# A two-layer decoder trunk: tokens 128 to 255 of layer 0 stored in reverse order

## Chip, cores and metric

The kernel runs on one core of a Trainium2 chip, in one launch. The metric is the device time of that launch in microseconds (us). All inputs and outputs are float32 in the chip's main memory.

## The reference

256 tokens of width 2048 pass through two layers and a last norm. Layer 0 mixes tokens by two recurrences side by side, layer 1 by attention; each layer ends with a squared-ReLU MLP. The change touches layer 0 alone:

```python
proj = rms_norm(x) @ w_in                       # 2048 -> 6144
x_lru, y_lru, q_h, f_h, v_h, g_h = jnp.split(proj, ...)
lru = rg_lru(causal_depthwise_conv(x_lru, ...)) * gelu(y_lru)     # 1024 wide
hg = hgrn2(q_h, f_h, v_h, g_h)                                    # 8 heads of 128
h = x + concatenate([lru, hg]) @ w_out
...
# hgrn2, per head, with q = silu(q_h), f = lb + (1 - lb) sigmoid(f_h), k = (1 - lb) sigmoid(-f_h):
decay = jnp.exp(b[:, :, :, None, :] - b[:, :, None, :, :])        # b: running sum of log f
scores = jnp.einsum('bhtk,bhsk,bhtsk->bhts', qc, kc, decay)       # causal: s <= t
o = jnp.einsum('bhts,bhsv->bhtv', scores, vc)
```

The score of query token t and key token s is a sum over 128 features, each with a decay of its own, the product of f over the tokens between them.

## The kernel before

**The stream of weights.** Nearly all the work is matrix products with streamed weights. A weight tile of 128x2048 (a unit) is loaded by SyncE (`raw`), rounded by ScalarE (ACT) into `hi`, and the rest `lo = raw - hi` is made by VectorE (DVE). TensorE (PE) multiplies three times: rounded activations by `hi` and by `lo`, the activations' rest by `hi`. `hi` and `lo` have three buffers each, so the rounding of a unit waits until PE has finished the unit three before it. In layer 0's input projection a unit is 24 matmuls of 512 columns; a group is four units and 512 output columns, in two PSUM tiles `p`, which ACT copies out to `tk`. The groups come in the order `v0 x0 x1 q0 G0 f0 q1 f1 G1 v1 g0 y0 g1 y1`, where G0 and G1 are the gates of the RG-LRU.

**The ticks.** The token mixing of layer 0 is cut into generator steps that are put between these matmuls. The table `TICKS` says, for every half unit, which lanes take a step: a and b are two pairs of HGRN2 heads each (`hgrn`), c the RG-LRU's inputs and outputs, e its scan (`lru_scan`), d the HGRN2's norm and output gate (`finish`). All of PE's matmuls are chained in the order in which the program writes them, and through layer 0's mixing so are DVE's and ACT's instructions (`InOrder`). What an engine does therefore stands in a fixed queue, and an instruction that waits holds up all behind it.

**The scores by levels.** `hgrn(c2)` handles two heads at once. Features lie on the partitions, 256 tokens along the row. Level c (1, 2, 4 to 128) joins pairs of neighbouring blocks of c tokens: keys of the first block meet queries of the second. Before level c each key has been multiplied by f of all tokens after it in its block and each query by f of all up to itself, so that one matmul gives the scores. Levels up to 16 run one matmul per head and half of the tokens (128 keys against the 64 queries in second blocks), so four per pair of heads; DVE puts the wanted blocks into the 128x128 score tiles `st` under a mask (`copy_predicated`). Levels 32 and 64 first gather the keys of first blocks of both halves into one contiguous tile `kc` (ACT), and run one matmul of 128 keys by 128 queries per head; ACT copies the blocks out to `st`. After each level DVE multiplies keys and queries by block products (`both_`) and forms the products of the next level (`nt`, in `xall`). Keys, queries and products lie in slots of the tile `xall`, so the profile calls all of these xall.

A step of lanes a and b stands every second tick, 24 matmuls apart: the transposed queries, the transposed forget gates (`f`), the diagonal (`pd`), and then the levels. Lanes a and b go through it twice: the first round is heads 0 to 3 (levels 1 to 32 at 140 to 177 us of the span), the second heads 4 to 7 (229 to 266 us). A step for both lanes together is called a block below. After level 128, the last step multiplies `st` by the values (`pd<-tk,st`).

Of the kernel before, what the change touches and what calls it, by code (L numbers as in the profile page):

```python
# [10 lines left out]
F32 = mybir.dt.float32  # L11
# [5 lines left out]
OP = mybir.AluOpType  # L17
# [3 lines left out]
P = 128  # L21
# [17 lines left out]


@with_exitstack
def trunk_kernel(ctx, tc, head, x, xtok, cols, tab, masks, pos, fin, w_in, w_gate, w_out, w_qkv, w_o, w1, w2, out):
# [361 lines left out]

    halfs.append(square(0))
    vfirst = tokens_group("v0", by_k=True, behind=halfs[1:])
    load = after(nc.sync.dma_start(xres[:, 1], xtok[:, 1]), loads)
    for d, f in ((tab_, tab), (msk, masks)):
        load = after(nc.sync.dma_start(d, f), [load])
    square(1)  # L410
# [80 lines left out]
    done = {"v0": vfirst}  # L491
    outs, roots, rooms = {}, {}, {}

    def turned(name, tiles, at):
        p = psc.tile([P, 2, S], F32, name=name, bufs=2 if name == "pl" else 1)
        for i, (z, m) in enumerate(zip(tiles, at)):
            for j in range(2):
                turn(p[:, i, j * P:j * P + P], z[:, j, m * P:m * P + P])
        return p

    def halves(t, c, second):
        return t.rearrange("p (n two c) -> p n two c", two=2, c=c)[:, :, int(second), :]

    def hgrn(c2):
        g, at = c2 // 2, 2 * (c2 % 2)
        bank = "pt" if at else "pd"
        heads = (2 * c2, 2 * c2 + 1)
        slot = 2048 * (c2 % 2)
        qk = xall[:, slot:slot + 1024].rearrange("p (t h s) -> p t h s", h=2, t=2)
        qp, kq = qk[:, 0], qk[:, 1]  # L510
        f = xall[:, slot + 1024:slot + 1536].rearrange("p (h s) -> p h s", h=2)
        rest = [slot + 1536]
        p = turned(bank, [done[f"q{g}"]] * 2, (at, at + 1))
        lut(qp, p, AF.Sigmoid)
        for h, hd in enumerate(heads):
            V.scalar_tensor_tensor(qp[:, h], p[:, h], omlb[:, hd:hd + 1], qp[:, h], op0=OP.mult, op1=OP.mult)
        yield
        p = turned("pl", [done[f"f{g}"]] * 2, (at, at + 1))
        lut(f, p, AF.Sigmoid)
        lut(kq, p, AF.Sigmoid, scale=-1.0)  # L520
        for h, hd in enumerate(heads):
            A.activation(f[:, h], f[:, h], AF.Identity, scale=omlb[:, hd:hd + 1], bias=lb[:, hd:hd + 1])
        yield
        pd = psc.tile([P, 2, 2, P], F32, name=bank, bufs=1)
        for h in range(2):
            for j in range(2):
                js = slice(j * P, j * P + P)
                mm(pd[:, h, j], kq[:, h, js], qp[:, h, js], start=True, stop=True)
        st = wk.tile([P, 2, 3, P], F32, name="st", bufs=2)
        V.tensor_tensor(st[:, :, :2], pd, ident[:, None, None, :].to_broadcast([P, 2, 2, P]), OP.mult)  # L530
        stf = st[:, :, :2].rearrange("p h a b -> p h (a b)")
        V.tensor_tensor(qp, qp, f, OP.mult)
        c = 1
        tot = f
        while c <= 128:
            yield
            pl = psc.tile([P, 2, 2, 64], F32, name="pl", bufs=2)
            plf = pl.rearrange("p h j c -> p h (j c)")
            if c == 128:
                for h in range(2):  # L540
                    mm(plf[:, h], kq[:, h, :P], qp[:, h, P:], start=True, stop=True)
                A.copy(st[:, :, 2], plf)
                break
            if c >= 32:
                for h in range(2):
                    mm(plf[:, h], kc[:, h], halves(qp[:, h], c, True), start=True, stop=True)
            else:
                for h in range(2):
                    for j in range(2):
                        js = slice(j * P, j * P + P)  # L550
                        mm(pl[:, h, j], kq[:, h, js], halves(qp[:, h, js], c, True), start=True, stop=True)
            if c <= 16:
                lv = LEVELS.index(c)
                V.copy_predicated(stf.rearrange("p h (n two c) -> p h n two c", two=2, c=c)[:, :, :, 1],
                                  msk[:, lv].rearrange("p (n c) -> p n c", c=c)[:, None].to_broadcast([P, 2, P // c, c]),
                                  pl.rearrange("p h j (n c) -> p h (j n) c", c=c))
            else:
                for n in range(P // c):
                    j, at_ = divmod(2 * n * c, P)
                    ns = slice(n * c, n * c + c)  # L560
                    A.copy(st[at_:at_ + c, :, j, at_ + c:at_ + 2 * c], plf[ns, :, ns])
            n = S // (2 * c)
            tt = tot.rearrange("p h (n two) -> p h n two", two=2)
            both_ = bass.AP(tensor=qk.tensor, offset=qk.offset + c,
                            ap=[list(qk.ap[0]), [2 * S - c, 2], [2 * c, 2 * n], [1, c]])
            fac = bass.AP(tensor=tot.tensor, offset=tot.offset,
                          ap=[list(tot.ap[0]), [1, 2], [2, 2 * n], [0, c]])
            V.tensor_tensor(both_, both_, fac, OP.mult)
            nt = xall[:, rest[0]:rest[0] + 2 * n].rearrange("p (h n) -> p h n", h=2)
            rest[0] += 2 * n  # L570
            V.tensor_tensor(nt, tt[:, :, :, 0], tt[:, :, :, 1], OP.mult)
            tot = nt
            c *= 2
            if c in (32, 64):
                at_ = slot + 1024 + 256 * (c == 64)
                kc = xall[:, at_:at_ + 256].rearrange("p (h s) -> p h s", h=2)
                A.copy(kc.rearrange("p h (n c) -> p h n c", c=c),
                       kq.rearrange("p h (n two c) -> p h n two c", two=2, c=c)[:, :, :, 0])
        yield
        vg = done[f"v{g}"]  # L580
        po = psc.tile([P, 2, 2, P], F32, name=bank, bufs=1)
        for h in range(2):
            vs = slice((at + h) * P, (at + h) * P + P)
            mm(po[:, h, 0], st[:, h, 0], vg[:, 0, vs], start=True, stop=True)
            mm(po[:, h, 1], st[:, h, 2], vg[:, 0, vs], start=True, stop=False)
            mm(po[:, h, 1], st[:, h, 1], vg[:, 1, vs], start=False, stop=True)
        if not at:
            roots[g] = wk.tile([P, 8], F32, name="hs", bufs=2)
        o = wk.tile([P, 2, 2, P], F32, name="ho", bufs=4)
        for h in range(2):  # L590
            for j in range(2):
                n = 2 * (at + h) + j
                A.activation(o[:, h, j], po[:, h, j], AF.Square, accum_out=roots[g][:, n:n + 1])
            outs[heads[h]] = o[:, h]
        A.copy(o, po)
        yield

    def finish(g, half):
# [6 lines left out]
        pair_ = [2 * half, 2 * half + 1]  # L605
        for at in pair_:
            o, z = outs[4 * g + at], done[f"g{g}"][:, :, at * P:at * P + P]
            s = wk.tile([P, 2, P], F32, name="g", bufs=2)
            lut(s, z, AF.Sigmoid)
            V.tensor_tensor(s, s, z, OP.mult)  # L610
            for j in range(2):
                V.scalar_tensor_tensor(o[:, j], o[:, j], roots[g][:, 2 * at + j:2 * at + j + 1], s[:, j],
                                       op0=OP.mult, op1=OP.mult)
        yield
        p = turned("po", [outs[4 * g + at] for at in pair_], (0, 0))
        if g and not half:
            bufb.tiles[3] = act.tile([P, 4, 2 * S], F32R, name="bufb3")
        for i, at in enumerate(pair_):
# [4 lines left out]

    def lru_in(n, half):
        b0 = 4 * n + 2 * half
        p = turned("po", [done[f"x{n}"]] * 2, (2 * half, 2 * half + 1))
# [51 lines left out]

    def lru_out(n, half):
        b0 = 4 * n + 2 * half  # L680
        p = turned("pt" if half else "pd", [done[f"y{n}"]] * 2, (2 * half, 2 * half + 1))
# [524 lines left out]
def _tables():  # L1206
# [27 lines left out]
def _layout(a):  # L1234
# [21 lines left out]
    for g in range(0, 16, 4):  # L1256
# [9 lines left out]
    return {  # L1266
        "head": c(head), "x": c(xf[:, 8:]),
        "xtok": c(n(a["x"]).reshape(2, P, D).transpose(1, 0, 2)),
        "cols": c(np.concatenate(cols, axis=1)),
        "tab": tab, "masks": masks,  # L1270
        "pos": c(n(a["positions"]).reshape(2, P).T),
# [23 lines left out]
```

## Time and profile before

| | |
|---|---|
| median of 3 runs | 2126.55 us (2126.04 to 2126.66) |
| the profiled execution | 2126.42 us |
| its span in the profile | 2124.6 us |
| PE, matmuls busy | 2115.1 us (100%) |
| DVE busy | 1780.3 us (84%) |
| ACT busy | 1310.4 us (62%) |
| granted TensorE clock | 0.999 of full speed |

The span is the time from the first to the last instruction that the profile shows; the execution's own time is 1.8 us longer. PE is TensorE's matmuls, PEld its weight loads, which overlap them. An arrow `p<-hi,bufa` means that tile p is written from hi and bufa. Line L241 is the helper `mm`, L244 the helper `turn` (a transpose on PE), and L68 the helper through which all DVE and ACT instructions go. A float32 matmul shows as two rows, since PE makes two passes of it. In a timeline a row has its start, its length and what it does; a number in brackets is the idle time of that engine before it and what ended it.

### The profile page before, as it was taken

Reading aid. Unit: us, or ns where it says so; the run is one execution under the profiler, and the core shown is the slowest. Engines: PE = TensorE matmul, PEld = TensorE weight load, DVE = VectorE, ACT = ScalarE, POOL = GpSimd, SP = SyncE. Lnnn points to the kernel's source line nnn. Section 1 sums busy time; section 2 is a strip of 40 time slices with the busy share of each in tenths; the row PEclk is TensorE's granted clock in tenths of the full one; section 3 lists DMA queues with packets and bytes.
Section 4 is the critical chain, followed back from the end, with each engine's and each line's share of the span. In section 5 each row is a group of like instructions: output and inputs, shape, how many; then the busy total and the mean of one; then the engine's idle time right before and its main releaser. Section 6 shows DMA issues by size and latency. Waiting matters only on the chain.

```text
span 2124.6 us, 24870 instructions
## 1 busy us (share of the span) xinstructions
PE 2115.1 (100%) x9828; PEld 1762.8 (83%) x9828; DVE 1780.3 (84%) x1687; ACT 1310.4 (62%) x1325; POOL 72.3 (3%) x89
## 2 busy tenths in 40 slices
PE   9999999999999999999999999999999999999998
PEld 8888888888888888888888888888888888888887
DVE  7676768988888888888998888798988987988897
ACT  7556466666566466566665666566755655755664
POOL 0000000000000000000000000000000000000000
PEclk9999999999999999999999999999999999999999
DMA  8544446887888878787788667567788778787885
GB/s 344 179 165 152 159 180 216 240 271 242 246 249 261 250 243 258 257 255 231 249 262 249 218 208 231 196 220 242 235 252 279 234 244 271 242 256 239 271 263 158
DMA packets 70164, 500.12 MB, mean 235 GB/s; under 512 B 7840, under 2 KB 8096, under 8 KB 10272
## 3 DMA queue, kind: packets, MB, share of 16 engines
q1 hardware_dynamic: 57888, 412.99, 51.1%
q0 software_dynamic: 11872, 84.94, 21.7%
q8 instruction: 77, 1.26, 0.2%
q10 hardware_dynamic: 288, 0.61, 0.1%
q14 instruction: 39, 0.32, 0.0%
HBM read 496.41 MB, written 2.10 MB: 235 GB/s over the span
## 4 chain that ended last, share of the span: by engine, by line
PE 98%; DVE 1%; ACT 1%; DMA 0%; issue 0%
PE p L241 61%; PE pd L241 15%; PE po L241 14%; PE pt L241 3%; PE pl L244 2%; PE pl L241 2%; ACT hi L68 0%; DVE lo L68 0%; DMA both_in<-in_head 0%; ACT tk L68 0%; DVE tk L68 0%; PE po L244 0%; DVE ho L68 0%; PE pd L244 0%; DVE g L68 0%
## 5 line engine op out<-in xcount | busy, mean ns | idle before, releaser
L68 DVE TENSOR_TENSOR lo<-raw,hi 128x2048 fp32r<-128x2048 f32 (+1 forms) x364 | 789.3, 2172 | 233.5 <-ACT hi L68 232.3
L68 ACT CAST hi<-raw 128x2048 fp32r<-128x2048 f32 (+1 forms) x364 | 659.3, 1817 | 500.6 <-PE p L241 309.5
L241 PE MATMUL p<-hi,bufa 128*128 128x512 f32 x2000 | 643.5, 393 | 0.2 <-ACT bufa L68 0.2
L241 PEld LDWEIGHTS p<-hi,bufa 128*128 128x128 f32 x2000 | 375.5, 188 | 77.6 <-ACT bufa L68 0.4
L241 PE MATMUL p<-hi,bufb 128*128 128x512 f32 x1264 | 405.0, 391 | 0.0
L241 PE MATMUL p<-lo,bufa 128*128 128x512 f32 x1000 | 389.4, 389 | 0.0
L68 DVE TENSOR_TENSOR lo<-s,hi 128x2048 fp32r<-128x2048 f32 x120 | 274.3, 2286 | 11.4 <-ACT hi L68 8.8
L241 PEld LDWEIGHTS p<-hi,bufb 128*128 128x128 f32 x1264 | 237.3, 188 | 48.8
L68 ACT CAST hi<-s 128x2048 fp32r<-128x2048 f32 x120 | 229.6, 1913 | 51.6 <-PE po L241 22.5
L241 PE MATMUL p<-lo,bufb 128*128 128x512 f32 x632 | 246.0, 389 | 0.0
L241 PEld LDWEIGHTS p<-lo,bufa 128*128 128x128 f32 x1000 | 187.9, 188 | 38.0 <-DVE lo L68 0.3
L241 PEld LDWEIGHTS p<-lo,bufb 128*128 128x128 f32 x632 | 118.7, 188 | 24.3
L241 PE MATMUL pd<-hi,bufa 128*128 128x512 f32 x352 | 116.8, 393 | 0.0
L241 PE MATMUL p<-hi,formx 128*128 128x512 f32 x352 | 116.3, 391 | 0.0
L68 DVE TENSOR_TENSOR lo<-t,hi 128x2048 fp32r<-128x2048 f32 x40 | 91.5, 2288 | 15.8 <-ACT hi L68 15.8
L241 PE MATMUL po<-hi,bufb 128*128 128x512 f32 (+1 forms) x320 | 102.4, 386 | 0.0
L241 PE MATMUL p<-hi,formh 128*128 128x512 f32 x288 | 94.5, 389 | 0.0
L68 DVE TENSOR_TENSOR s<-s,raw 128x2048 f32<-128x2048 f32 x40 | 91.3, 2284 | 0.5 <-DMA raw<-in_w_qkv 0.5
L68 DVE TENSOR_TENSOR s<-raw,t 128x2048 f32<-128x2048 f32 x40 | 91.5, 2286 | 0.2 <-DMA raw<-in_w_o 0.2
L68 ACT ACTIVATE y<-y 128x512 f32<-128x512 f32 x112 | 68.8, 629 | 28.0 <-DVE y L68 27.2
L241 PE MATMUL po<-hi,bufa 128*128 128x512 f32 x256 | 84.9, 393 | 0.0
L68 ACT CAST hi<-t 128x2048 fp32r<-128x2048 f32 x40 | 76.5, 1914 | 11.7 <-PE pd L241 6.0
(296 smaller groups left out, 2789.1 us busy)
## 6 DMA issues: line engine op xcount, KB each, us to landing
raw<-in_w SPq DMA_DIRECT2D x224, 1024.0 KB, 6.6
raw<-in_w_in SPq DMA_DIRECT2D x45, 1024.0 KB, 4.8
raw<-in_w_qkv SPq DMA_DIRECT2D x42, 1024.0 KB, 6.7
t<-in_w SPq DMA_DIRECT2D x32, 1024.0 KB, 6.8
t<-in_w POOLq DMA_DIRECT2D x32, 1024.0 KB, 8.9
s<-in_w POOLq DMA_DIRECT2D x32, 1024.0 KB, 9.2
raw<-in_w_out SPq DMA_DIRECT2D x15, 1024.0 KB, 4.9
raw<-in_w_o SPq DMA_DIRECT2D x15, 1024.0 KB, 4.8
```

What stands on the lines that cost most here:

```text
L68: i = call(*args, **kw)
L241: chain[:] = [after(T.matmul(*args, **kw), chain)]
L244: chain[:] = [after(T.transpose(out_, in_, ident), chain)]
```

## The change

Tokens 128 to 255 are stored backwards through layer 0's mixing: the host reverses them in the features' copy of x and in `xback` (1 MB, loaded in the place of the second half of `xtok`). In the reversed half the later block of a pair comes first. The layout of keys and queries is set so that at each level the wanted keys of both halves can be gathered into one tile `kc` of 128 columns, and the 64 queries of each half are read by one access pattern: levels 1 to 16 now run as 32 and 64 did, one matmul per head with 128 keys by 128 queries. For this ACT gathers `kc` at every level (two copies of 128 elements per lane, the function `gather`), and the sigmoid of the keys is written in two halves. The masked copies of levels 1 to 16 become two of half the size, one for each half of the tokens. `both_` now stands ahead of the masked copies. The transposes of `turned(..., back=True)` (in `lru_in`, `lru_out` and `finish`) write the second half in reverse, so that the RG-LRU and the output projection see the tokens in order. `finish` takes its scratch tile from pool tmp (`z`) and no longer from wk (`g`). The order of PE's matmuls for the weights and the ticks are unchanged.

```diff
-    load = after(nc.sync.dma_start(xres[:, 1], xtok[:, 1]), loads)
+    load = after(nc.sync.dma_start(xres[:, 1], xback), loads)
...
     done = {"v0": vfirst}
     outs, roots, rooms = {}, {}, {}
 
-    def turned(name, tiles, at):
+    def turned(name, tiles, at, back=False):
         p = psc.tile([P, 2, S], F32, name=name, bufs=2 if name == "pl" else 1)
         for i, (z, m) in enumerate(zip(tiles, at)):
             for j in range(2):
-                turn(p[:, i, j * P:j * P + P], z[:, j, m * P:m * P + P])
+                to = p[:, i, j * P:j * P + P]
+                turn(to[:, ::-1] if back and j else to, z[:, j, m * P:m * P + P])
         return p
-
-    def halves(t, c, second):
-        return t.rearrange("p (n two c) -> p n two c", two=2, c=c)[:, :, int(second), :]
 
     def hgrn(c2):
         g, at = c2 // 2, 2 * (c2 % 2)
...
         heads = (2 * c2, 2 * c2 + 1)
         slot = 2048 * (c2 % 2)
         qk = xall[:, slot:slot + 1024].rearrange("p (t h s) -> p t h s", h=2, t=2)
-        qp, kq = qk[:, 0], qk[:, 1]
+        view = lambda t, at_, *dims: bass.AP(tensor=t.tensor, offset=t.offset + at_, ap=[list(t.ap[0])] + [list(d) for d in dims])
+        queries = view(qk, 0, (S, 2), (2 * S + P, 2), (1, P))
+        keys = (qk[:, 1, :, :P], qk[:, 0, :, P:])
         f = xall[:, slot + 1024:slot + 1536].rearrange("p (h s) -> p h s", h=2)
+        by_half = lambda t: t.rearrange("p h (j s) -> p h j s", j=2)
         rest = [slot + 1536]
         p = turned(bank, [done[f"q{g}"]] * 2, (at, at + 1))
-        lut(qp, p, AF.Sigmoid)
+        lut(queries, by_half(p), AF.Sigmoid)
         for h, hd in enumerate(heads):
-            V.scalar_tensor_tensor(qp[:, h], p[:, h], omlb[:, hd:hd + 1], qp[:, h], op0=OP.mult, op1=OP.mult)
+            V.scalar_tensor_tensor(queries[:, h], by_half(p)[:, h], omlb[:, hd:hd + 1], queries[:, h], op0=OP.mult, op1=OP.mult)
         yield
         p = turned("pl", [done[f"f{g}"]] * 2, (at, at + 1))
         lut(f, p, AF.Sigmoid)
-        lut(kq, p, AF.Sigmoid, scale=-1.0)
+        for j in range(2):
+            lut(keys[j], by_half(p)[:, :, j], AF.Sigmoid, scale=-1.0)
         for h, hd in enumerate(heads):
             A.activation(f[:, h], f[:, h], AF.Identity, scale=omlb[:, hd:hd + 1], bias=lb[:, hd:hd + 1])
+        kc = wk.tile([P, 2, P], F32, name="kc", bufs=2)
+
+        def gather(c):
+            pairs_ = lambda t: t.rearrange("p h (n two c) -> p h n two c", two=2, c=c)
+            for j in range(2):
+                A.copy(pairs_(kc)[:, :, :, j], pairs_(keys[j])[:, :, :, j])
+
         yield
         pd = psc.tile([P, 2, 2, P], F32, name=bank, bufs=1)
         for h in range(2):
             for j in range(2):
-                js = slice(j * P, j * P + P)
-                mm(pd[:, h, j], kq[:, h, js], qp[:, h, js], start=True, stop=True)
+                mm(pd[:, h, j], keys[j][:, h], queries[:, h, j], start=True, stop=True)
         st = wk.tile([P, 2, 3, P], F32, name="st", bufs=2)
+        V.tensor_tensor(queries, queries, by_half(f), OP.mult)
+        gather(1)
         V.tensor_tensor(st[:, :, :2], pd, ident[:, None, None, :].to_broadcast([P, 2, 2, P]), OP.mult)
-        stf = st[:, :, :2].rearrange("p h a b -> p h (a b)")
-        V.tensor_tensor(qp, qp, f, OP.mult)
         c = 1
         tot = f
-        while c <= 128:
+        while True:
             yield
-            pl = psc.tile([P, 2, 2, 64], F32, name="pl", bufs=2)
-            plf = pl.rearrange("p h j c -> p h (j c)")
-            if c == 128:
+            pl = psc.tile([P, 2, P], F32, name="pl", bufs=2)
+            if c == P:
                 for h in range(2):
-                    mm(plf[:, h], kq[:, h, :P], qp[:, h, P:], start=True, stop=True)
-                A.copy(st[:, :, 2], plf)
+                    mm(pl[:, h], qk[:, 1, h, :P], qk[:, 1, h, P:], start=True, stop=True)
+                A.copy(st[:, :, 2], pl)
                 break
-            if c >= 32:
-                for h in range(2):
-                    mm(plf[:, h], kc[:, h], halves(qp[:, h], c, True), start=True, stop=True)
-            else:
-                for h in range(2):
-                    for j in range(2):
-                        js = slice(j * P, j * P + P)
-                        mm(pl[:, h, j], kq[:, h, js], halves(qp[:, h, js], c, True), start=True, stop=True)
-            if c <= 16:
-                lv = LEVELS.index(c)
-                V.copy_predicated(stf.rearrange("p h (n two c) -> p h n two c", two=2, c=c)[:, :, :, 1],
-                                  msk[:, lv].rearrange("p (n c) -> p n c", c=c)[:, None].to_broadcast([P, 2, P // c, c]),
-                                  pl.rearrange("p h j (n c) -> p h (j n) c", c=c))
-            else:
-                for n in range(P // c):
-                    j, at_ = divmod(2 * n * c, P)
-                    ns = slice(n * c, n * c + c)
-                    A.copy(st[at_:at_ + c, :, j, at_ + c:at_ + 2 * c], plf[ns, :, ns])
+            for h in range(2):
+                mm(pl[:, h], kc[:, h], view(qk, h * S + c, (2 * S + P - c, 2), (2 * c, 64 // c), (1, c)),
+                   start=True, stop=True)
             n = S // (2 * c)
             tt = tot.rearrange("p h (n two) -> p h n two", two=2)
-            both_ = bass.AP(tensor=qk.tensor, offset=qk.offset + c,
-                            ap=[list(qk.ap[0]), [2 * S - c, 2], [2 * c, 2 * n], [1, c]])
-            fac = bass.AP(tensor=tot.tensor, offset=tot.offset,
-                          ap=[list(tot.ap[0]), [1, 2], [2, 2 * n], [0, c]])
-            V.tensor_tensor(both_, both_, fac, OP.mult)
+            both_ = view(qk, c, (2 * S - c, 2), (2 * c, 2 * n), (1, c))
+            V.tensor_tensor(both_, both_, view(tot, 0, (1, 2), (2, 2 * n), (0, c)), OP.mult)
+            if c < 64:
+                gather(2 * c)
+            for j in range(2):
+                if c <= 16:
+                    to = st[:, :, j].rearrange("p h (n two c) -> p h n two c", two=2, c=c)[:, :, :, 1 - j]
+                    m = msk[:, LEVELS.index(c), 64 * j:64 * j + 64].rearrange("p (n c) -> p n c", c=c)
+                    V.copy_predicated(to, m[:, None].to_broadcast([P, 2, 64 // c, c]),
+                                      pl[:, :, 64 * j:64 * j + 64].rearrange("p h (n c) -> p h n c", c=c))
+                    continue
+                for i in range(64 // c):
+                    k0, q0 = (2 * i + j) * c, (2 * i + 1 - j) * c
+                    A.copy(st[k0:k0 + c, :, j, q0:q0 + c], pl[k0:k0 + c, :, 64 * j + i * c:64 * j + i * c + c])
             nt = xall[:, rest[0]:rest[0] + 2 * n].rearrange("p (h n) -> p h n", h=2)
             rest[0] += 2 * n
             V.tensor_tensor(nt, tt[:, :, :, 0], tt[:, :, :, 1], OP.mult)
             tot = nt
             c *= 2
-            if c in (32, 64):
-                at_ = slot + 1024 + 256 * (c == 64)
-                kc = xall[:, at_:at_ + 256].rearrange("p (h s) -> p h s", h=2)
-                A.copy(kc.rearrange("p h (n c) -> p h n c", c=c),
-                       kq.rearrange("p h (n two c) -> p h n two c", two=2, c=c)[:, :, :, 0])
         yield
         vg = done[f"v{g}"]
         po = psc.tile([P, 2, 2, P], F32, name=bank, bufs=1)
...
-            s = wk.tile([P, 2, P], F32, name="g", bufs=2)
+            s = tmp.tile([P, S], F32, name="z").rearrange("p (j c) -> p j c", j=2)
...
-        p = turned("po", [outs[4 * g + at] for at in pair_], (0, 0))
+        p = turned("po", [outs[4 * g + at] for at in pair_], (0, 0), back=True)
...
-        m = (s // (2 * c_) == col // c_) & (s % (2 * c_) < c_)
-        masks[:, lv, :64] = m
-        masks[:, lv, 64:] = m
+        for j in range(2):
+            masks[:, lv, 64 * j:64 * j + 64] = (s // (2 * c_) == col // c_) & (s // c_ % 2 == j)
...
-    xf = n(a["x"]).reshape(S, KB, P).transpose(2, 1, 0)
+    xs = n(a["x"]).reshape(2, P, D)
+    xback = xs[1, ::-1]
+    xf = np.concatenate([xs[0], xback]).reshape(S, KB, P).transpose(2, 1, 0)
```

Three places in the queues, as the built programs have them (shapes are those of the output).

PE, level 1 of the first round, before: eight 64-column matmuls (two heads, two halves, two lanes) among those of the weights.

```order
L241 MATMUL p<-hi,bufa 128x512
L241 MATMUL pl<-xall 128x64 x8
L241 MATMUL p<-hi,bufa 128x512
L241 MATMUL p<-lo,bufa 128x512
L241 MATMUL p<-hi,bufa 128x512 x2
```

PE at the same place after:

```order
L241 MATMUL p<-hi,bufa 128x512
L241 MATMUL pl<-xall,kc 128x128 x4
L241 MATMUL p<-hi,bufa 128x512
L241 MATMUL p<-lo,bufa 128x512
L241 MATMUL p<-hi,bufa 128x512 x2
```

The four matmuls of 128 columns stand where the eight of 64 stood.

ACT, first round, from the cast that follows the forget gates to the gather for level 32, before:

```order
L68 CAST hi<-raw 128x2048 x3
L68 ACTIVATE tk<-p,nr_319 128x512 x2
L68 CAST hi<-raw 128x2048 x2
L68 CAST hi<-raw 128x1024 x2
L68 COPY xall<-xall 128x256 x2
L68 CAST hi<-raw 128x2048
```

ACT at the same place after:

```order
L68 CAST hi<-raw 128x2048
L68 COPY kc<-xall 128x128 x4
L68 CAST hi<-raw 128x2048
L68 COPY kc<-xall 128x64x2 x4
L68 CAST hi<-raw 128x2048
L68 COPY kc<-xall 128x32x4 x4
L68 ACTIVATE tk<-p,nr_319 128x512 x2
L68 CAST hi<-raw 128x2048
L68 COPY kc<-xall 128x16x8 x4
L68 CAST hi<-raw 128x2048
L68 COPY kc<-xall 128x8x16 x4
L68 CAST hi<-raw 128x1024 x2
```

Four gathering copies (two per lane) now stand between each two casts of the weights.

DVE, first round, level 1, before:

```order
L68 TENSOR_TENSOR lo<-raw,hi 128x2048
L68 COPY_PREDICATED st<-msk,pl 128x2x128
L68 TENSOR_TENSOR xall<-xall 128x2x256
L68 TENSOR_TENSOR xall<-xall 128x256
L68 COPY_PREDICATED st<-msk,pl 128x2x128
L68 TENSOR_TENSOR xall<-xall 128x2x256
L68 TENSOR_TENSOR xall<-xall 128x256
```

DVE at the same place after:

```order
L68 TENSOR_TENSOR lo<-raw,hi 128x2048
L68 TENSOR_TENSOR xall<-xall 128x2x256
L68 COPY_PREDICATED st<-msk,pl 128x2x64 x2
L68 TENSOR_TENSOR xall<-xall 128x256
L68 TENSOR_TENSOR xall<-xall 128x2x256
L68 COPY_PREDICATED st<-msk,pl 128x2x64 x2
L68 TENSOR_TENSOR xall<-xall 128x256
```

`both_` (128x2x256) moved ahead of the masked copies, which became two; `lo` of the weights still stands ahead of both lanes.

More of the change, by code (lines that the diff above doesn't have):

```diff
@@ L41, in trunk_kernel @@
 @with_exitstack
-def trunk_kernel(ctx, tc, head, x, xtok, cols, tab, masks, pos, fin, w_in, w_gate, w_out, w_qkv, w_o, w1, w2, out):
+def trunk_kernel(ctx, tc, head, x, xtok, xback, cols, tab, masks, pos, fin, w_in, w_gate, w_out, w_qkv, w_o, w1, w2, out):
     nc = tc.nc
@@ L625, in lru_in @@
         b0 = 4 * n + 2 * half
-        p = turned("po", [done[f"x{n}"]] * 2, (2 * half, 2 * half + 1))
+        p = turned("po", [done[f"x{n}"]] * 2, (2 * half, 2 * half + 1), back=True)
         for i in range(2):
@@ L680, in lru_out @@
         b0 = 4 * n + 2 * half
-        p = turned("pt" if half else "pd", [done[f"y{n}"]] * 2, (2 * half, 2 * half + 1))
+        p = turned("pt" if half else "pd", [done[f"y{n}"]] * 2, (2 * half, 2 * half + 1), back=True)
         z = outs[f"y{n}"][:, half].rearrange("p (i s) -> p i s", i=2)
@@ L1267, in _layout @@
         "head": c(head), "x": c(xf[:, 8:]),
-        "xtok": c(n(a["x"]).reshape(2, P, D).transpose(1, 0, 2)),
+        "xtok": c(xs.transpose(1, 0, 2)), "xback": c(xback),
         "cols": c(np.concatenate(cols, axis=1)),
```

## The prediction

> **What bounds the kernel now.** I read the page first, then PE's waits, then PE's, ACT's and DVE's timelines through the two rounds of levels. The page and PE's waits (engine, tile and line, released by: us in total, times, longest):
>
> ```profile
> PE 2115.1 (100%) x9828; PEld 1762.8 (83%) x9828; DVE 1780.3 (84%) x1687; ACT 1310.4 (62%) x1325; POOL 72.3 (3%) x89
> PE po L301 <- DVE e L68: 1.1, 1, 1.1
> PE p L241 <- ACT bufa L68: 0.2, 1, 0.2
> ```
>
> PE waits 1.3 us in all. Work taken from PE shortens the kernel until another engine holds PE up; work added to ACT (62%) and DVE (84%) costs nothing until then. But the changed levels fill only some 75 us of the span, and there the two engines stand in fixed queues, so I look at that stretch and not at the shares.
>
> **What PE saves.** The blocks of levels 1 and 32 in the first round (start, length, what), with the weights' matmul behind each:
>
> ```profile
> 140.11 1.89 PE L241 MATMUL pl<-xall 128*128 128x64 f32 x16
> 141.81 0.48 PE L241 MATMUL p<-hi,bufa 128*128 128x512 f32 x1
> ...
> 176.41 1.05 PE L241 MATMUL pl<-xall 128*128 128x128 f32 x8
> 177.22 0.48 PE L241 MATMUL p<-hi,bufa 128*128 128x512 f32 x1
> ```
>
> Eight matmuls of 64 columns are 16 passes and take 141.81 - 140.11 = 1.70 us, 106 ns a pass. The four of 128 columns that replace them have the form of level 32's block: 8 passes, 0.81 us, 101 ns a pass. So a pass costs the same at half the width, and a block saves 0.89 us; five levels in two rounds make ten blocks, 8.9 us. The Trainium skill (TensorE: Matmul & The Clock Gate, section Back-to-back issue gap) gives an isolated matmul a gap of N/2.4 + 2.5 ns. By that, 16 x 29 ns would equal 8 x 56 ns and nothing would be saved; the 106 and 101 ns of these rows speak against it here.
>
> **What ACT and DVE gain to do.** ACT in the first round:
>
> ```profile
> 137.59 1.91 ACT L68 CAST hi<-raw 128x2048 fp32r<-128x2048 f32 x1 [4.61 <-PE p L241]
> ...
> 159.37 1.91 ACT L68 CAST hi<-raw 128x2048 fp32r<-128x2048 f32 x1 [4.75 <-PE p L241]
> 166.65 2.00 ACT L68 CAST hi<-raw 128x1024 fp32r<-128x1024 f32 x2 [5.36 <-PE p L241]
> ...
> 173.93 1.91 ACT L68 CAST hi<-raw 128x2048 fp32r<-128x2048 f32 x1 [1.24 <-PE p L241]
> ...
> 178.80 0.41 ACT L68 COPY xall<-xall 128x256 f32<-128x256 f32 x1 [0.90 <-DVE xall L68]
> 179.22 0.84 ACT L68 COPY st<-pl 32x64 f32<-32x64 f32 x4
> 180.08 0.41 ACT L68 COPY xall<-xall 128x256 f32<-128x256 f32 x1
> 180.50 1.26 ACT L68 ACTIVATE tk<-p,nr 128x512 f32<-128x512 f32 x2
> 181.65 1.90 ACT L68 CAST hi<-raw 128x2048 fp32r<-128x2048 f32 x1
> ```
>
> DVE there:
>
> ```profile
> 141.74 0.73 DVE L68 COPY_PREDICATED st<-msk,pl 128x256 f32<-128x256 int8 x1
> 142.26 1.06 DVE L68 TENSOR_TENSOR xall<-xall 128x512 f32<-128x512 f32 x2
> 143.23 0.74 DVE L68 COPY_PREDICATED st<-msk,pl 128x256 f32<-128x256 int8 x1
> ...
> 161.32 2.29 DVE L68 TENSOR_TENSOR lo<-raw,hi 128x2048 fp32r<-128x2048 f32 x1 [2.24 <-ACT hi L68]
> 163.53 0.43 DVE L68 COPY_PREDICATED st<-msk,pl 128x256 f32<-128x256 int8 x1
> 163.86 0.79 DVE L68 TENSOR_TENSOR xall<-xall 128x512 f32<-128x512 f32 x2
> 164.56 0.43 DVE L68 COPY_PREDICATED st<-msk,pl 128x256 f32<-128x256 int8 x1
> ...
> 170.21 0.44 DVE L68 COPY_PREDICATED st<-msk,pl 128x256 f32<-128x256 int8 x1
> ```
>
> Before, ACT's casts wait for PE, 4.6 to 5.4 us each, and come one per level, 166.65 - 159.37 = 7.28 us apart. With the shorter block PE wants one every 7.28 - 0.89 = 6.39 us. The change closes a loop that was open: ACT's gather for the next level waits for DVE's `both_` of this one, `both_` stands behind `lo`, `lo` waits for the cast, and the next cast stands behind the gathers. The loop never touches PE, so a faster PE doesn't shorten it. Its length, cast to cast, at level 8:
>
> - cast to `lo`: 161.32 - 159.37 = 1.95; `lo` to DVE's next: 163.53 - 161.32 = 2.21.
> - lane a: `both_` and `nt` 164.56 - 163.86 = 0.70, and two masked copies of half the size. No trace shows a half one. The whole takes 0.33 in step (163.86 - 163.53) and 0.52 at levels 1 and 2 (142.26 - 141.74). Bounds for one half: half of that (0.17, 0.26) and all of it (0.33, 0.52). I take 0.20, and 0.35 at levels 1 and 2, since each instruction has a fixed part. Lane a: 1.10.
> - lane b: `both_` to its end 0.69 with 0.03 for the signal, 0.72.
> - lane b's two gather copies of 128 elements, between (179.22 to 180.08)/4 = 0.21 for 64 elements and 180.50 - 180.08 = 0.42 for 256. In these rows each copy starts after the one before has ended. I take 0.31, so 0.62; lane a's two lie beside DVE's work.
>
> Sum 1.95 + 2.21 + 1.10 + 0.72 + 0.62 = 6.60 us at levels 4, 8 and 16; level 1, with 0.97 for `both_` and `nt` (143.23 - 142.26) and 0.70 for the masked copies, 7.17; level 2 with some 0.84 there, 7.04. Round 1's split cast of level 16 frees `both_` sooner: 170.21 - 166.65 = 3.56 where 163.53 - 159.37 = 4.16, so 6.00. Nearly all are above 6.39: **the loop, not PE, would set the pace.**
>
> **The start and end of each round.** ACT, the round's start in the first round, its end in both:
>
> ```profile
> 127.18 1.09 ACT L68 ACTIVATE xall<-pl 128x512 f32<-128x512 f32 x2 [0.67 <-PE pl L244]
> 128.15 1.09 ACT L68 ACTIVATE xall<-xall,lb,omlb 128x256 f32<-128x256 f32 x2
> ...
> 184.17 0.85 ACT L68 ACTIVATE bufb<-pl,c__91 128x256 f32<-128x256 f32 x2
> 184.88 0.87 ACT L68 ACTIVATE bufb<-p,c__91 128x256 f32<-128x256 f32 x2
> 186.02 0.84 ACT L68 ACTIVATE bufb<-pl,c__91 128x256 f32<-128x256 f32 x2 [0.27 <-PE pl L241]
> ...
> 189.21 1.09 ACT L68 COPY st<-pl 64x128 f32<-64x128 f32 x4 [0.55 <-PE pl L241]
> ...
> 226.78 1.91 ACT L68 CAST hi<-raw 128x2048 fp32r<-128x2048 f32 x1 [4.61 <-PE p L241]
> ...
> 269.90 0.47 ACT L68 ACTIVATE bufb<-po,c__91 128x256 fp32r<-128x256 f32 x1 [0.19 <-PE po L244]
> 271.30 1.26 ACT L68 ACTIVATE tk<-p,nr 128x512 f32<-128x512 f32 x2
> 272.44 1.91 ACT L68 CAST hi<-raw 128x2048 fp32r<-128x2048 f32 x1
> ```
>
> DVE, the diagonal's mask in round 1, the group norm's small instructions in round 2:
>
> ```profile
> 135.22 0.68 DVE L68 TENSOR_TENSOR st<-pd,tab__186 128x512 f32<-128x512 f32 x1
> 135.82 0.68 DVE L68 TENSOR_TENSOR xall<-xall 128x512 f32<-128x512 f32 x1
> ...
> 248.19 0.17 DVE L68 TENSOR_SCALAR hs<-hs 128x8 f32<-128x8 f32 x1
> ...
> 250.51 2.29 DVE L68 TENSOR_TENSOR lo<-raw,hi 128x2048 fp32r<-128x2048 f32 x1
> ```
>
> PE, level 128 in round 2:
>
> ```profile
> 278.79 1.05 PE L241 MATMUL pl<-xall 128*128 128x128 f32 x8
> ```
>
> The keys' sigmoid was one instruction of 512, 0.49 in step ((128.15 - 127.18)/2), and becomes two of 256 from PSUM, 0.36 each ((184.88 - 184.17)/2): 0.23 per lane. DVE's first four products then start at 135.22 + 0.46 = 135.68. The query's product of lane b is now the third of them (steps of 0.60) and ends at 135.68 + 2 x 0.60 + 0.68 = 137.56; gather(1) waits for it and takes 0.62; so the cast of 137.59 comes at 138.2.
>
> Round 1 adds up the loop, with the two copies to `tk` (181.65 - 180.50 = 1.15) behind level 2: 138.2 + 7.17 + 7.04 + 1.15 + 6.60 + 6.60 + 6.00 = 172.8 for level 32's cast (before 173.93; an unhindered PE would ask for it at 169.5). Then 1.95 + 2.21 + 0.68 = 4.84 to lane a's `both_`, and on ACT two gathers (0.62), four copies to `st` (0.85), both again for lane b, and the `tk` copies: 172.8 + 4.84 + 2.94 + 1.15 = 181.7, before 181.65. So round 1's 4.45 us are gone here: the next matmuls wait for ACT. ACT's idle 0.27 and 0.55 that follow are filled, which can give back 0.8 at most.
>
> Round 2: the cast at 226.78 comes at 226.78 + 0.6 - 0.8 = 226.6. + 7.17 + 7.04 + 1.15 + 6.60 = 248.6 for level 8. There twelve small DVE instructions (248.19 to 250.51) stand ahead of `lo` and hold it 0.2 longer (2.32, begun some 0.15 before the cast, against 1.95), and ACT has two more activations (0.7, a pair as at 184.17): + 6.60 + 0.9 = 256.1; + 6.60 = 262.7 for level 32; + 4.84 + 2.94 = 270.5; output copies (271.30 - 269.90 = 1.40) and `tk` (272.44 - 271.30 = 1.14): 273.0, before 272.44. The last level's matmuls need level 64's `both_`: 273.0 + 1.95 + 2.21 + 2 x 0.70 = 278.6, where they started at 278.79. The two rounds together come out at -0.2 us.
>
> **Edits with nothing on the path.** `xback` is as large as the half of `xtok` it replaces. Query instructions have other strides but the same count and elements. `finish` has its scratch in another pool, same sizes. `both_` ahead of the masked copies is in the loop already. The reversed transposes are bounded under rivals. Levels 32 to 128 keep their copies. No DMA queue is passed: SP and POOL lose and gain nothing.
>
> **Sum.** 2126.42 (the profiled execution) - 0.2 = 2126.2; that execution lies 0.13 below the median of the runs, so 2126.3. The unknown prices: 16 copies per round lie on the path (two at the start, ten in levels, four at level 32), so each 0.1 us on a copy is 3.2 us in all: -3.2 at 0.21, +3.5 at 0.42. Masked copies at half price give some -1, at whole price +2.9.
>
> **The rivals.** *The loop stays shorter than PE's 6.39, and the saving comes through.* Against: 6.60 to 7.17 by the rows. For: ACT's activations overlap by 0.1 in step (1.09 for a pair that steps 0.97), and small copies might. At 0.17 a copy the loop is 6.32, and 32 x 0.14 = 4.5 us come back: 2121.8, and 2117.5 if all 8.9 did. It decides below 0.18 a copy.
>
> *Strided gathers are dear, and the kernel is slower.* DVE's masked copies cost 0.52 for 0.33 at runs of one and two tokens; a gather reads and writes such runs on ACT. With that factor, 0.50 a copy, the loop is 6.98 and more and PE waits longer than it saved: 32 x 0.19 = 6.1, 2132.4. Against: level 32's copies show nothing of the kind, and levels 8 and 16 have long runs. It passes the bound at 0.31 + (4.25 + 0.2)/32 = 0.45 a copy.
>
> *Reversed writes slow the transposes.* Eight in order:
>
> ```profile
> 126.54 1.03 PE L244 MATMUL pl<-tab__186,tk 128*128 128x128 f32 x8
> ```
>
> That is 0.13 each at most. 24 become reversed; at twice the time, +3.1: 2129.4, still within the bound. The Trainium skill (SBUF — State Buffer, section Door 1: The DMA port swizzle) says PSUM has lines of 8 bytes and that access out of sequence there slows matmuls significantly. No run here shows a reversed write; a reversed row still uses both words of such a line one after the other.
>
> *PE saves nothing* (a pass costs by its columns): the loop then lies under 7.28, and only the ends' half microsecond is left, 2126.9.
>
> **How the numbers follow.** A measurement of this kernel can tell about 0.2% (4.25 us) from no change: 2122.3 to 2130.8. Forecast, the loop eats the gain: 0.50, at 2126.3, its own range from -3.2 and -1 to +3.5 cut to 2122.3 to 2130. The saving comes through: 0.20, beyond the bound. Dear gathers: 0.22, beyond it on the other side. Reversed transposes 0.05, and no saving on PE 0.03, both within. So faster 0.20, same 0.58, slower 0.22. A range of 2121.5 to 2131.5 leaves out 0.1 of each outer rival.
>
> **What would show it.** Blocks `pl<-xall,kc` of 0.8 us and gather copies of 0.31 would bear out the two prices. PE's waits, 1.3 us before, should grow by some 8.6 in total, released by ACT at the blocks of levels 8 to 64, at `pd<-tk,st` and at `p` behind level 32, and casts should stand next to gathers with no wait for PE. ACT still idling 3 us and more on PE before each cast would make the forecast wrong towards faster; gathers near 0.5, with PE waiting at every level, towards slower.

## The result and the profile after

| | before | changed |
|---|---|---|
| median | 2126.59 us (22 runs, 2125.64 to 2127.35) | 2123.07 us (22 runs, 2121.32 to 2124.34) |
| profiled execution | 2126.42 us | 2122.04 us |
| its span | 2124.6 us | 2120.2 us |

The ratio is 0.9983, with a 95% interval of 0.9976 to 0.9990: 3.5 us faster, which is clear of the noise, yet under the 0.2% bound and inside the range. The profiled execution, 4.4 us below that of before, is at the lower end of its runs; the last experiment shows most of the reason.

PE's blocks of levels 1 and 32 in round 1, and of levels 32, 64 and 128 in round 2, after (columns as before):

```profile
140.34 1.07 PE L241 MATMUL pl<-xall,kc 128*128 128x128 f32 x8
141.16 0.48 PE L241 MATMUL p<-hi,bufa 128*128 128x512 f32 x1
...
172.17 1.05 PE L241 MATMUL pl<-xall,kc 128*128 128x128 f32 x8
...
258.24 0.61 PE L241 MATMUL pl<-xall,kc 128*128 128x128 f32 x4
259.10 0.71 PE L241 MATMUL pl<-xall,kc 128*128 128x128 f32 x4 [0.25 <-ACT kc L68]
...
266.55 0.71 PE L241 MATMUL pl<-xall,kc 128*128 128x128 f32 x4 [0.35 <-ACT st L68]
268.65 0.50 PE L241 MATMUL p<-hi,bufa 128*128 128x512 f32 x1 [1.39 <-ACT tk L68]
...
274.22 1.18 PE L241 MATMUL pl<-xall 128*128 128x128 f32 x8
```

Level 32 of round 2 in before:

```profile
265.60 1.05 PE L241 MATMUL pl<-xall 128*128 128x128 f32 x8
```

A block takes 0.82 us (141.16 - 140.34). PE starts 0.23 late (140.11 before) and is 4.24 early at level 32 (176.41 before): the whole 4.47 of five blocks has come through by then. At level 1 of round 2 it is 2.89 early (226.41, where before had 229.30), at level 32 there 7.36 (258.24, 265.60 before), and at level 128 it is 4.57 early (278.79 before). So what PE loses, it loses at the **end** of each round, 1.35 and 2.79 us, not level by level. PE's waits over the kernel name it:

```profile
PE p L241 <- ACT tk L68: 1.8, 2, 1.4
PE po L301 <- DVE e L68: 1.1, 1, 1.1
PE pl L241 <- ACT st L68: 0.3, 1, 0.3
PE pd L241 <- ACT st L68: 0.3, 1, 0.3
PE pl L241 <- ACT kc L68: 0.2, 1, 0.2
```

ACT's casts in round 1, with the gathers behind level 4 and the work from level 32's gather to the next unit:

```profile
137.96 1.91 ACT L68 CAST hi<-raw 128x2048 fp32r<-128x2048 f32 x1
...
144.80 1.91 ACT L68 CAST hi<-raw 128x2048 fp32r<-128x2048 f32 x1
...
152.65 1.90 ACT L68 CAST hi<-raw 128x2048 fp32r<-128x2048 f32 x1
157.56 0.50 ACT L68 COPY kc<-xall 128x128 f32<-128x128 f32 x2 [3.01 <-DVE xall L68]
158.70 0.50 ACT L68 COPY kc<-xall 128x128 f32<-128x128 f32 x2 [0.63 <-DVE xall L68]
159.10 1.90 ACT L68 CAST hi<-raw 128x2048 fp32r<-128x2048 f32 x1
...
165.51 1.99 ACT L68 CAST hi<-raw 128x1024 fp32r<-128x1024 f32 x2
...
171.13 1.90 ACT L68 CAST hi<-raw 128x2048 fp32r<-128x2048 f32 x1
176.04 0.50 ACT L68 COPY kc<-xall 128x128 f32<-128x128 f32 x2 [3.01 <-DVE xall L68]
176.44 0.84 ACT L68 COPY st<-pl 32x64 f32<-32x64 f32 x4
177.31 0.50 ACT L68 COPY kc<-xall 128x128 f32<-128x128 f32 x2
177.82 0.85 ACT L68 COPY st<-pl 32x64 f32<-32x64 f32 x4
178.68 1.26 ACT L68 ACTIVATE tk<-p,nr 128x512 f32<-128x512 f32 x2
179.83 1.90 ACT L68 CAST hi<-raw 128x2048 fp32r<-128x2048 f32 x1
```

No cast waits for PE in these rounds any more; each follows the gathers (behind level 2 also the copies to `tk`), which wait 3 us for DVE. The loop is there, 165.51 - 159.10 = 6.41 us long against PE's 6.34 or so. By itself this link, 0.07 over PE's pace, would cost next to nothing. From cast to cast the links of round 1 are 6.84, 7.85 (the `tk` copies are in it), 6.45, 6.41, 5.62 and 8.70, 41.87 us together; with all gathers on DVE (an experiment below) ACT goes from the same cast to the same cast in 176.68 - 137.92 = 38.76. It is level 1, level 2 with the `tk` copies and the stretch behind level 32 that make ACT late, and PE meets it where the casts' lead is used up, at the round's end. Behind level 32, ACT works from 176.04 to 179.83 almost without a gap.

DVE at levels 1 and 8, and the gather copies of the whole kernel (duration in ns: least, median, most):

```profile
142.71 0.74 DVE L68 COPY_PREDICATED st<-msk,pl 128x128 f32<-128x128 int8 x2
143.23 1.06 DVE L68 TENSOR_TENSOR xall<-xall 128x256 f32<-128x256 f32 x2
...
163.84 0.49 DVE L68 COPY_PREDICATED st<-msk,pl 128x128 f32<-128x128 int8 x2
164.23 0.79 DVE L68 TENSOR_TENSOR xall<-xall 128x32 f32<-128x32 f32 x2
```

```profile
L68 ACT COPY kc<-xall x56: 292/298/313, 136.3 to 265.3; 128x128 f32<-128x128 f32 x56
```

A gather copy lasts 0.298 us in the middle, 0.313 at most, at short runs of tokens as at long ones. But two in a row overlap: lane b's pair takes 159.10 - 158.70 = 0.40 up to the cast, not 0.62. The two masked halves take 164.23 - 163.84 = 0.39 at level 8 and 143.23 - 142.71 = 0.52 at level 1; the whole copies took 0.33 and 0.52.

### The profile page after: what moved, and what is told of

Its sections match the earlier page's. It is cut to its first block, busy times and chain, and to the rows that moved or that the text cites. A ratio compares the mean times of both kernels' runs of the same rounds, so it can differ in the third digit from the quotient of the medians.

```text
span 2120.2 us, 24809 instructions
## 1 busy us (share of the span) xinstructions
PE 2108.1 (99%) x9748; PEld 1754.5 (83%) x9748; DVE 1780.6 (84%) x1707; ACT 1319.6 (62%) x1377; POOL 72.3 (3%) x89
## 4 chain that ended last, share of the span: by engine, by line
PE 94%; ACT 2%; DVE 2%; issue 1%; DMA 0%; SPq 0%; DVEq 0%; ACTq 0%
PE p L241 59%; PE pd L241 15%; PE po L241 14%; PE pt L241 3%; PE pl L244 2%; ACT hi L68 1%; PE pl L241 1%; DVE lo L68 1%; DVE xall L68 0%; DMA both_in<-in_head 0%; ACT bufb L68 0%; ACT tk L68 0%; ACT bufa L68 0%; ACT kc L68 0%; DVE tk L68 0%
```

## The experiments

Seven kernels were run with five rounds beside the kernel before (2126.45 us median in the first four, 2126.49 in the others), and the changed kernel three times more for its profile. The diffs are shortened: `...` and the comments stand for code left out.

**PE's saving taken away.** Two matmuls of 64 columns per head instead of one of 128:

```diff
-                mm(pl[:, h], kc[:, h], view(...), start=True, stop=True)
+                for j in range(2):      # levels 1 to 16
+                    mm(pl[:, h, 64 * j:64 * j + 64], kc[:, h], view(...)[:, j], start=True, stop=True)
```

> The changed kernel, with the scores of levels 1 to 16 again taken in two matmuls of 64 columns per head (same gathered keys, queries of one half each), so that PE saves nothing and all else stays. Theory (the loop of ACT's gathers and DVE sets the pace, PE's shorter blocks are the only gain): PE's period is 7.27 us again, above the loop's 6.41, so levels 1 to 16 hold nothing up; only the longer ACT work at level 32 costs 0.3 to 1 us a round. 2126.9 to 2128.5. Rival 1 (the gain of the changed kernel comes from the layout, the order on DVE or the transposes, not from PE's blocks): about 2123. Rival 2 (gathers are free beside an unhurried PE, at level 32 too): 2126.6.

Measured: 2126.92 us, ratio 1.0002 (0.9993 to 1.0011). PE waits for nothing but the 1.1 us that it waited before. ACT's cast behind level 32 in round 1, at 181.65 before:

```profile
182.94 1.90 ACT L68 CAST hi<-raw 128x2048 fp32r<-128x2048 f32 x1
```

1.29 us late, but still ahead of PE's need, which is why it ends at the lower edge of the first theory's figure. The first rival falls: without the shorter blocks nothing is gained. The second rival (gathers free beside an unhurried PE, 2126.6) can't be told from the theory by a time of 2126.92; that PE waits for nothing new speaks for it. The rest of the change costs about nothing when PE takes 7.27 us a level.

**Gathers on DVE.**

```diff
-                A.copy(pairs_(kc)[:, :, :, j], pairs_(keys[j])[:, :, :, j])
+                V.tensor_copy(pairs_(kc)[:, :, :, j], pairs_(keys[j])[:, :, :, j])
```

> The changed kernel with the gather copies on DVE (behind both_) in the place of ACT. Theory: the loop is cut, since ACT's casts no longer stand behind copies that wait for DVE; DVE has room (per level 2.2 of lo, 2.2 of level work, some 0.8 of copies against PE's 6.35). Nearly all of the 8.9 us comes through: 2117.5 to 2119, PE's waits below 2 us. Rival 1 (the missing 5 us are lost at PE's banks or in the reversed transposes, whoever gathers): 2122 to 2123. Rival 2 (DVE, at 84%, becomes the late engine): 2124 or more.

Measured: 2118.86 us, ratio 0.9965 (0.9952 to 0.9977). ACT's cast of level 32 waits for PE again, as before the change (169.75 where 173.93 stood), and beside the 1.1 us of before PE waits once, 0.9 us at `pl` for ACT's `st`:

```profile
169.75 1.91 ACT L68 CAST hi<-raw 128x2048 fp32r<-128x2048 f32 x1 [4.34 <-PE p L241]
```

The theory holds: both rivals' times are missed, and PE has no new wait for DVE.

**Every gather twice.**

```diff
+                for _ in range(2):
-                A.copy(pairs_(kc)[:, :, :, j], pairs_(keys[j])[:, :, :, j])
+                    A.copy(pairs_(kc)[:, :, :, j], pairs_(keys[j])[:, :, :, j])
```

> The changed kernel with every gather copy made twice on ACT. Theory: eight pairs of copies per round lie on the path (start, levels 2 to 32 of lane b, both lanes at 64), 0.41 us a pair, so 16 x 0.41 = 6.6 us more than 2123.1: 2129 to 2130. Rival (the casts have slack and the copies lie beside other work): at most 2 us more, 2123 to 2125.

Measured: 2134.35 us, ratio 1.0034 (1.0022 to 1.0047); 11.3 us above the changed kernel where 6.6 was expected. The copies are on the path, but the sum missed two things. ACT from level 4's cast to level 8's:

```profile
162.12 1.90 ACT L68 CAST hi<-raw 128x2048 fp32r<-128x2048 f32 x1
166.99 2.25 ACT L68 COPY kc<-xall 128x128 f32<-128x128 f32 x8 [2.96 <-DVE xall L68]
169.15 2.00 ACT L68 CAST hi<-raw 128x1024 fp32r<-128x1024 f32 x2
```

Lane a's copies now reach into lane b's, so the loop is 169.15 - 162.12 = 7.03, 0.62 more and not 0.41. And PE at the end of round 2, with the stretches around it (start and end, length, busy us of PE, PEld, DVE, ACT and POOL, granted clock, DMA share and GB/s):

```profile
276.66 0.71 PE L241 MATMUL pl<-xall,kc 128*128 128x128 f32 x4 [1.33 <-ACT st L68]
278.76 0.79 PE L241 MATMUL p<-hi,bufa 128*128 128x512 f32 x1 [1.39 <-ACT tk L68]
```

```profile
274.00:278.00 4.00, 2.00 (x11) 1.19 (x9) 0.48 (x1) 3.27 (x13) 0.00 (x0) 1.00 0.54 229
278.00:282.00 4.00, 3.24 (x8) 2.57 (x9) 1.38 (x2) 3.95 (x8) 0.00 (x0) 0.51 0.00 0
282.00:284.00 2.00, 2.00 (x6) 1.56 (x5) 2.00 (x4) 0.77 (x3) 0.00 (x0) 0.50 0.00 0
```

After two waits close together the granted clock falls to half for some 6 us; (1 - 0.51) x 4 + (1 - 0.50) x 2 = 3.0 us of clock are lost, and the 2 us behind still show 0.76. No theory had that in it. The one of the five runs with a mean clock of 0.999 took 2130.88 us; the others, at 0.997 and 0.998, took 2134.28 to 2135.24.

**Gathers of levels 2 to 16 left out.**

```diff
-            if c < 64:
+            if 16 <= c < 64:
                 gather(2 * c)
```

> The changed kernel without the gathers for levels 2 to 16 (those levels use the keys gathered for level 1, so their scores are not the reference's). Theory: ACT's casts wait only for PE in levels 1 to 16 and the blocks' saving comes through up to level 32, where ACT's copies still take back up to 1 us a round: 2118 to 2120. Rival (the saving is lost elsewhere): 2122 to 2123.

Measured: 2118.72 us, ratio 0.9964 (0.9952 to 0.9977). The casts wait for PE again, here behind level 2:

```profile
157.22 1.91 ACT L68 CAST hi<-raw 128x2048 fp32r<-128x2048 f32 x1 [3.86 <-PE p L241]
```

The theory holds. With the gathers moved off ACT or left out, the time is the same.

**Masked copies ahead of `both_`.**

```diff
-            V.tensor_tensor(both_, ...)
-            if c < 64:
-                gather(2 * c)
             for j in range(2): ...      # masked copies, copies to st
+            V.tensor_tensor(both_, ...)
+            if c < 64:
+                gather(2 * c)
```

> The changed kernel with both_ and the gather behind the masked copies, as both_ stood before the change. Theory (the loop runs over DVE's both_ of lane b): lane b's two masked copies come into the loop, 0.40 us at levels 4 to 16 and 0.52 at 1 and 2, 2.24 a round and 4.5 in all on top of 2123.1: 2126.5 to 2128. Rival (only ACT's own work counts, DVE's order does not): 2122.5 to 2123.5.

Measured: 2125.48 us, ratio 0.9996 (0.9987 to 1.0005): 2.4 us above the changed kernel, so DVE's order counts and the rival falls, but 4.5 was expected. The loop grew as said, and some of it came back at level 32:

```profile
160.98 1.90 ACT L68 CAST hi<-raw 128x2048 fp32r<-128x2048 f32 x1
...
167.82 2.00 ACT L68 CAST hi<-raw 128x1024 fp32r<-128x1024 f32 x2
...
173.84 1.90 ACT L68 CAST hi<-raw 128x2048 fp32r<-128x2048 f32 x1
175.65 0.84 ACT L68 COPY st<-pl 32x64 f32<-32x64 f32 x4
178.75 0.50 ACT L68 COPY kc<-xall 128x128 f32<-128x128 f32 x2 [2.27 <-DVE xall L68]
...
181.79 1.90 ACT L68 CAST hi<-raw 128x2048 fp32r<-128x2048 f32 x1
```

167.82 - 160.98 = 6.84, 0.43 over 6.41. At level 32 lane a's copies to `st` now run while ACT waits for `both_`: 181.79 - 173.84 = 7.95 where the changed kernel needs 179.83 - 171.13 = 8.70. That is 0.75 back of the 2.4 us by which the links of round 1 grew, and as much in round 2. The two profiled executions, both with a full clock, lie 2125.47 - 2122.04 = 3.4 us apart; the medians lie closer, since part of the changed kernel's runs lose time to its clock (last experiment), while all eleven here show 0.999.

**Gathers on DVE, and lane b's copies of level 32 too.**

```diff
-                    A.copy(st[k0:k0 + c, ...], pl[...])
+                    (V.tensor_copy if at and c == 32 else A.copy)(st[k0:k0 + c, ...], pl[...])
```

> Gathers on DVE as in the run with gathers on DVE, and level 32's four block copies of lane b to st on DVE too. Theory: what that run left is ACT's eight copies at level 32 ahead of tk and the next cast (a PE wait of 0.9 us, and some 1.2 us that the casts lose between level 32 and the next unit); 0.85 us less on ACT gives 0.4 to 1.2 us more: 2117.6 to 2118.5. Rival (DVE's copies hold lo up instead): 2118.9 or more.

Measured: 2118.97 us, ratio 0.9965 (0.9952 to 0.9977): no better than with the gathers alone, and the same 0.9 us wait of PE on `st`. The theory of what was left is wrong in that point. The time is the rival's, but its cause isn't shown: PE waits 0.2 us for `lo` here, and 0.1 us between the two runs means nothing. In both, PE's wait at level 32 of round 2 ends where ACT's four copies of lane a to `st` end (257.60 + 0.84 = 258.44 and PE at 258.50; here 258.27 + 0.84 = 259.11 and PE at 259.16). The copies moved here were lane b's, which come behind that wait.

**Lane a's gathers on ACT, lane b's on DVE.**

```diff
-                A.copy(pairs_(kc)[:, :, :, j], pairs_(keys[j])[:, :, :, j])
+                (V.tensor_copy if at else A.copy)(pairs_(kc)[:, :, :, j], pairs_(keys[j])[:, :, :, j])
```

> The changed kernel with lane b's gathers on DVE, lane a's on ACT. Theory: ACT then waits only for lane a's both_; cast to cast 1.95 + 2.21 + 0.6 + 0.03 + 0.41 = 5.2 us, below PE's 6.35, so PE sets the pace as with all gathers on DVE: 2118.3 to 2119.5. Rival (ACT's casts must not wait for DVE at all, one lane is enough to hold them): 2120.5 to 2122.

Measured: 2118.82 us, ratio 0.9964 (0.9952 to 0.9977). The casts wait for PE a little, and PE waits for nothing new:

```profile
156.80 0.50 ACT L68 COPY kc<-xall 128x128 f32<-128x128 f32 x2 [3.02 <-DVE xall L68]
157.64 1.91 ACT L68 CAST hi<-raw 128x2048 fp32r<-128x2048 f32 x1 [0.35 <-PE p L241]
```

So it is lane b's turn in the loop that made it too long. This version and the one with all gathers on DVE beat both kernels: their runs, 2117.99 to 2120.89, all lie below those of the changed kernel.

**The changed kernel again.**

> The changed kernel again, for a profile. Its times spread over 3 us (2121.3 to 2124.3), the kernel before over 1.7. Theory: PE's waits at the end of round 2 (0.35 and 1.39 us some 2 us apart) sometimes bring the granted clock down for a few us, as in the run with every copy twice (0.50 for 6 us after waits of 1.33 and 1.39). A run at 2123 us or more then shows a stretch of clock 0.5 between 265 and 280 us and a mean clock of 0.998, one below 2122.8 none. Rival: the spread comes from the loads at the start; then the clock is full between 130 and 300 us in every run, and the times differ in the first 50 us.

> As the run before it: a time of 2123 us or more goes with a stretch of clock 0.5 between 265 and 280 us, a time below 2122.8 us with none; by the rival neither does.

> As the two runs before it: a time of 2123 us or more goes with a stretch of clock 0.5 between 265 and 280 us, a time below 2122.8 us with none; by the rival neither does.

Measured: 2123.84, 2124.70 and 2123.91 us, each with a mean clock of 0.998. All three are above 2123 us, and all three show the stretch of half clock. The first of them, PE's wait and the stretches around it:

```profile
268.40 0.80 PE L241 MATMUL p<-hi,bufa 128*128 128x512 f32 x1 [1.39 <-ACT tk L68]
```

```profile
266.00:270.00 4.00, 2.31 (x8) 1.85 (x9) 0.97 (x2) 3.41 (x7) 0.00 (x0) 0.80 0.28 119
270.00:272.00 2.00, 2.00 (x7) 1.59 (x6) 1.25 (x1) 1.93 (x6) 0.00 (x0) 0.55 0.00 0
```

The profiled execution of 2122.04 us has the same waits and a full clock there:

```profile
266.00:270.00 4.00, 2.26 (x12) 1.66 (x12) 0.97 (x2) 3.40 (x8) 0.00 (x0) 1.00 0.33 137
270.00:272.00 2.00, 2.00 (x11) 1.65 (x10) 0.99 (x1) 1.93 (x6) 0.00 (x0) 1.00 0.00 0
```

The first run lacks 0.20 x 4 + 0.45 x 2 = 1.7 us of clock there. PE's own steps give nearly the same price: from the matmul behind the wait (268.65 in the execution with the full clock; 268.40, 268.52 and 269.02 in the three) to the last step's `pd<-tk,st` (280.72; 281.91, 282.04 and 282.55) it takes 12.07 us with the full clock and 13.51 to 13.53 in the three, 1.45 more. That the first run ended 1.8 us later is a coincidence of several things: it was 0.25 us early before the stretch, and later, like the second, it waited 0.9 to 1.0 us for a `lo`, behind a DVE instruction that waited 2.0 and 2.1 us for a weight load to land (0.5 with the full clock, 0.7 in the third run). The third had no such wait, was 0.37 us late before the stretch, and ended 1.87 us later.

The theory holds in all three, but no new run below 2122.8 us was had. The 22 runs first measured add that side by their mean clocks: all ten up to 2122.7 us have 0.999; of the twelve from 2123.0 on eight have 0.998 and four 0.999. So the clock makes much of the spread. The rival falls as the main cause; loads still make part of it.

## Why the prediction was right, and where it was off

- *PE saves 0.89 us a block, 8.9 in all*: right, 4.47 for five blocks in round 1 and as much in round 2 (7.36 - 2.89).
- *The loop of ACT's gathers and DVE closes and eats the gain*: right in mechanism, too large in size. The runs with the gathers moved, split between the engines or left out all come to 2118.7 to 2118.9, where PE's saving stands almost whole; the changed kernel, with the loop in it, gains 3.5. The forecast had it gain 0.2, so that "same" came true with 0.7 us to spare.
- *Its length, 6.60*: 0.2 too long, and that is the step that was mis-sized. The copies of 0.31 were taken to follow each other without overlap, as the copies in `xall` do; a pair takes 0.40 instead of 0.62. Every link of round 1 came out shorter than the sum had it: 6.84, 7.85, 6.45, 6.41, 5.62 and 8.70 against 7.17, 8.19, 6.60, 6.60, 6.00 and 8.93, 1.6 us in all. The prediction's own price (3.2 us for each 0.1 us on a copy) makes 0.11 x 32 = 3.5 us of it, and 2126.3 - 3.5 = 2122.8 is next to the 2123.07 measured. That closeness is partly luck: in the three executions above 2123 us that were profiled the half clock costs 1.45 us, which was in no term.
- *The masked halves, 0.20 each and 0.35 at levels 1 and 2*: 0.20 at level 8, as taken, 0.26 at level 1. Lane a's two at two levels in two rounds are 8 x 0.09 = 0.7 us; with them the sum comes to 2122.1, where the execution with the full clock was 2122.04.
- *Round 1's 4.45 us are gone, since the cast behind level 32 comes no earlier than before*: the sum gave that cast no lead over PE and only ACT's idle 0.8 us back. In the run without PE's saving it came 1.29 us later than before and PE didn't wait; in the changed kernel it came 1.82 earlier (181.65 - 179.83) and PE kept 2.89.
- *Dear strided gathers*: wrong; 292 to 313 ns over all levels.
- *Reversed transposes*: no cost seen. `finish`'s transposes, half of them reversed, took 272 ns in the mean before and after:

```profile
L244 PE MATMUL po<-tab__186,ho 128*128 128x128 f32 x16 | 2.4, 272 | 0.0
```

- *PE's waits grow by 8.6 and stand at levels 8 to 64, at `pd<-tk,st` and at `p` behind level 32*: off in size. The listed waits grew by 2.4 in the profile. PE lost 1.35 + 2.79 = 4.1, since a step over a wait is longer than the idle time listed: behind level 32 of round 1 the step over a wait of 0.39 takes 179.42 - 178.75 = 0.67, where before the same step took 0.12. Levels 8 and 16 show no wait. `p` behind level 32 (0.39) and `pd<-tk,st` (0.3) came true in round 1, the blocks of levels 32 and 64 in round 2 (0.25 and 0.35). The largest, 1.39 at `p` behind level 64 of round 2, was not among them.
- *The rival by which the saving comes through* was half right: its ground, the overlap of small instructions on ACT, is what moved the time, but it stopped short of the 0.17 a copy that it needed.

## What to carry to other kernels

Before shortening the engine that bounds, look for loops between the other engines that it has been covering: an in-order queue that must wait for another queue, whose input it produces, has a length of its own, and a saving is worth only the distance down to it. Add up all its links over the stretch, and the lead that the bounding engine's inputs have: here two links lay next to PE's pace, and the three long ones cost the time. Then cut the loop where it is long, here by moving one lane's copies to the engine that makes their input; the same PE saving became 7.7 us instead of 3.5. In a sum over many small instructions the step from one start to the next matters, not the duration, and whether two overlap is to be taken from rows of the same kind of pair.

## What was not expected of the hardware

After PE waits of 0.35 and 1.39 us within 3 us (PE busy for 2.3 of the 4 us from 266 to 270) the granted clock was at half for some 3.4 us in three executions, and not in a fourth with the same waits; after waits of 1.33 and 1.39 us (busy for 2.0 of 4) it was there for 6 us. The Trainium skill (TensorE: Matmul & The Clock Gate, section Why this matters for your kernels) asks for no idle gap over some 3 us. In these traces the half clock follows two shorter gaps close together; no gap of 3 us stands before it. That the gaps brought it is argued from their place, since no run changed them alone. The same page (section What's actually happening) has the clock set by a free-running window of activity, and a run-to-run difference with the same waits agrees with that, though no run here shows the window itself.

The share of busy time alone doesn't decide it. The run with every gather twice had waits of 1.66 and 1.05 us at the end of round 1, too, with PE busy for less than half of the stretch, and kept its full clock:

```profile
180.00:185.00 5.00, 2.28 (x18) 1.88 (x16) 0.94 (x4) 4.53 (x18) 0.00 (x0) 1.00 0.54 210
```

On ACT, two copies of 128 elements into `kc`, 0.298 us each, are through in 0.40 up to the next start, while single copies of 256 in `xall` took their full 0.42 in the profile before.
